# A softmax over rows of 512: ten transfers in place of sixteen, and a new order on VectorE

## The chip, the cores and the metric

The kernel runs on one core of one Trainium2 chip. The core has five engines that run side by side: TensorE (PE, not used here), VectorE (DVE), ScalarE (ACT), GpSimd (POOL) and SyncE (SP), which here only issues transfers. Transfers between the large memory (HBM) and the on-chip buffer (SBUF, 128 partitions) are carried out by 16 DMA engines, each of which works through the packets of eight partitions in the order in which SP issued the transfers.

The metric is the device time of one execution in microseconds. Each kernel is timed several times; the median counts.

## The reference

```python
def setup_inputs():
    batch, seq, dim = 16, 1024, 512
    return {"x": np.random.randn(batch, seq, dim).astype(np.float32)}

def reference(x):
    x_max = np.max(x, axis=-1, keepdims=True)
    exp_x = np.exp(x - x_max)
    return (exp_x / np.sum(exp_x, axis=-1, keepdims=True)).astype(np.float32)
```

There are 16,384 rows of 512 floats (2 KB each). Every row is read once and written once: 33.55 MB in, 33.55 MB out.

## The kernel before, in words

The rows are cut into 8 chunks. In a chunk every partition holds 16 rows that follow each other in HBM, 32 KB in one run, so a chunk is 128 x 16 rows, 4.19 MB. The buffer `held` has six places for chunks; chunks 6 and 7 take the places of chunks 0 and 1 once these are stored. A chunk is worked in two groups of 8 rows per partition, so there are 16 groups, and every instruction of VectorE and GpSimd handles one group.

A group goes through four steps:

- maximum (`rowmax`, line 133, VectorE): the negated maximum of each of the 8 rows. The first group of a chunk waits for the chunk's load.
- exponential (line 165, ScalarE): eight instructions, one for each row of the group; each subtracts the maximum, takes the exponential in place and sums it. After the eighth the semaphore `expd` goes up by one.
- reciprocal of the sums (line 142, VectorE), which waits for `expd`.
- multiply in place (line 144): on GpSimd for groups 0 to 11, on VectorE for the groups in `ON_VECTOR`, 12 to 15. It waits for the reciprocal. A chunk's store waits until both of its groups are multiplied.

No scheduler decides the order; it is written out for each engine. SP issues, in this order, the loads of chunks 0 to 5 (line 112, the first ahead of the program's opening barrier), stores 0 to 2, loads 6 and 7 (line 124, each after the store of the chunk whose place it takes), stores 3 to 7 (line 127). SP stands still at each wait, and whatever is behind in its list stands too. VectorE runs the maximum of group g, then the reciprocal of group g-1 and, where it is VectorE's, the multiply of g-1. ScalarE and GpSimd take groups in order. The two loops of ScalarE (`exps`) are there because the place in `held` starts again after 12 groups.

`take` (line 94) is a wait for a semaphore that also takes the count down, so the profile names line 94 wherever an engine waits.

Of the kernel before, what the change touches and what calls it, by code (L numbers as in the profile page):

```python
# [1 line left out]

# [4 lines left out]

F32 = mybir.dt.float32
EXP = mybir.ActivationFunctionType.Exp
AX = mybir.AxisListType.X  # L10

CHUNK = 16
CHUNKS = 8
PLACES = 6
GROUP = 8
PER = CHUNK // GROUP
GROUPS = CHUNKS * PER
RING = PLACES * PER  # L20


ORDER = [("L", k) for k in range(PLACES)] + [
    ("S", 0),
    ("S", 1),
    ("S", 2),
    ("L", 6),
    ("L", 7),
    ("S", 3),
    ("S", 4),  # L30
    ("S", 5),
    ("S", 6),
    ("S", 7),
]


ON_VECTOR = (12, 13, 14, 15)


AT_HEAD = {mybir.EngineType.SP: 1}  # L40

def loads_at_the_head(nc):

    main, body = nc.main_func.blocks[0], nc.main_func.blocks[1]
    for engine, count in AT_HEAD.items():
        loads = [
            i
            for i in body.instructions  # L50
            if i.engine == engine and type(i).__name__ == "InstDMACopy"
        ][:count]
        barrier = next(
            n
            for n, i in enumerate(main.instructions)
            if i.engine == engine and type(i).__name__ == "InstDrain"
        )
        for load in loads:
            body.instructions.remove(load)
        main.instructions[barrier:barrier] = loads  # L60


@with_exitstack
def kernel(
    ctx: ExitStack,
    tc: tile.TileContext,
    x: bass.AP,
    out: bass.AP,
):
    nc = tc.nc  # L70
    nc.at_finalize(loads_at_the_head)
    P = nc.NUM_PARTITIONS

    x_rows = x.flatten_outer_dims().rearrange("(c p r) d -> c p r d", p=P, r=CHUNK)
    out_rows = out.flatten_outer_dims().rearrange("(c p r) d -> c p r d", p=P, r=CHUNK)
    n, _, _, d = x_rows.shape
    assert n == CHUNKS

    held = nc.alloc_sbuf_tensor("held", [P, PLACES * CHUNK, d], F32).ap()
    shift = nc.alloc_sbuf_tensor("shift", [P, GROUPS * GROUP], F32).ap()  # L80
    sums = nc.alloc_sbuf_tensor("sums", [P, GROUPS * GROUP], F32).ap()
    recip = nc.alloc_sbuf_tensor("recip", [P, GROUPS * GROUP], F32).ap()

    loaded = [nc.alloc_semaphore(f"loaded{k}") for k in range(CHUNKS)]
    stored = [nc.alloc_semaphore(f"stored{k}") for k in range(CHUNKS)]
    maxed = nc.alloc_semaphore("maxed")
    expd = nc.alloc_semaphore("expd")
    to_pool = nc.alloc_semaphore("to_pool")
    to_vector = nc.alloc_semaphore("to_vector")
    scaled = [nc.alloc_semaphore(f"scaled{k}") for k in range(CHUNKS)]  # L90

    def take(engine, semaphore, n):

        engine.wait_ge(semaphore, n).then_inc(semaphore, -n)  # L94

    def place(k):
        at = (k % PLACES) * CHUNK
        return held[:, at : at + CHUNK, :]

    def rows(g):  # L100
        at = (g % RING) * GROUP
        return held[:, at : at + GROUP, :]

    def stats(t, g):
        return t[:, g * GROUP : (g + 1) * GROUP]

    with tc.manual_schedule():  # L110
        for _, k in ORDER[:PLACES]:
            first = nc.sync.dma_start(out=place(k), in_=x_rows[k])
            first.then_inc(loaded[k], 16)
            tc.no_tile_sem_insts.add(first.ins.name)
    tc.close()
    tc.compile()  # L116

    reused = set()
    for what, k in ORDER[PLACES:]:
        if what == "L":  # L120
            if k >= PLACES:
                take(nc.sync, stored[k - PLACES], 16)
                reused.add(k - PLACES)
            nc.sync.dma_start(out=place(k), in_=x_rows[k]).then_inc(loaded[k], 16)
        else:
            take(nc.sync, scaled[k], PER)
            nc.sync.dma_start(out=out_rows[k], in_=place(k)).then_inc(stored[k], 16)


    def rowmax(g):  # L130
        if g % PER == 0:
            take(nc.vector, loaded[g // PER], 16)
        nc.vector.reduce_max(  # L133
            out=stats(shift, g), in_=rows(g), axis=AX, negate=True
        ).then_inc(maxed, 1)

    def scale(g):
        engine, ready = (
            (nc.vector, to_vector) if g in ON_VECTOR else (nc.gpsimd, to_pool)
        )  # L140
        take(nc.vector, expd, 1)
        nc.vector.reciprocal(out=stats(recip, g), in_=stats(sums, g)).then_inc(ready, 1)  # L142
        take(engine, ready, 1)
        engine.tensor_mul(  # L144
            out=rows(g),
            in0=rows(g),
            in1=stats(recip, g).unsqueeze(2).to_broadcast([P, GROUP, d]),
        ).then_inc(scaled[g // PER], 1)

    for g in range(GROUPS):  # L150
        rowmax(g)
        if g:
            scale(g - 1)
    scale(GROUPS - 1)


    nc.scalar.preload_act_table(EXP)  # L157

    def exps(first, turns):
        with nc.scalar.Fori(0, turns) as i:  # L160
            take(nc.scalar, maxed, 1)
            for r in range(GROUP):
                row = held[:, bass.ds(i * GROUP + r, 1), :]
                at = bass.ds(i * GROUP + (first * GROUP + r), 1)
                act = nc.scalar.activation(  # L165
                    out=row,
                    in_=row,
                    func=EXP,
                    bias=shift[:, at],
                    scale=1.0,  # L170
                    accum_out=sums[:, at],
                )
            act.then_inc(expd, 1)

    exps(0, RING)
    exps(RING, GROUPS - RING)


    for k in range(CHUNKS):
        if k not in reused:  # L180
            take(nc.sync, stored[k], 16)


# [1 line left out]
_INS = ['x']  # L185
_OUTS = [((16, 1024, 512), 'float32')]


# [23 lines left out]
```

## Time and profile before

| | us |
|---|---|
| median of three runs | 160.24 (160.07 to 160.30) |
| the profiled execution's own time | 160.32 |
| its span, first to last instruction | 159.0 |
| VectorE busy | 90.6 |
| ScalarE busy | 92.0 |
| GpSimd busy | 84.0 |
| 16 maxima on VectorE, mean of one | 4.398 |
| 12 multiplies on GpSimd, mean of one | 7.018 |
| 4 multiplies on VectorE, mean of one | 4.576 |
| 128 exponentials, each with the read of its sum behind it, mean of one | 0.706 and 0.186 |

The span is what the trace of one execution covers; the device time holds a little more than the span. In the trace's rows, "busy" is the time in which an engine ran instructions; a transfer's "us to landing" goes from its issue on SP to the last of its semaphore updates, and so holds the time that it stood behind other transfers. The DMA share of a stretch is the packets' time over 16 engines' time; a packet's time and bytes are counted where it starts and ends, so in stretches of one microsecond both figures jump about, and a long stretch is steadier. "x" gives the number of instructions.

### The profile page before, as it was taken

Reading aid. Unit: us, or ns where it says so; the run is one execution under the profiler, and the core shown is the slowest. Engines: PE = TensorE matmul, PEld = TensorE weight load, DVE = VectorE, ACT = ScalarE, POOL = GpSimd, SP = SyncE. Lnnn points to the kernel's source line nnn. Section 1 sums busy time; section 2 is a strip of 40 time slices with the busy share of each in tenths; the row PEclk is TensorE's granted clock in tenths of the full one; section 3 lists DMA queues with packets and bytes.
Section 4 is the critical chain, followed back from the end, with each engine's and each line's share of the span. In section 5 each row is a group of like instructions: output and inputs, shape, how many; then the busy total and the mean of one; then the engine's idle time right before and its main releaser. Section 6 shows DMA issues by size and latency. Waiting matters only on the chain. (4 is left out here: it accounts for less than half of the span.)

```text
span 159.0 us, 740 instructions
## 1 busy us (share of the span) xinstructions
DVE 90.6 (57%) x36; ACT 92.0 (58%) x257; POOL 84.0 (53%) x16
## 2 busy tenths in 40 slices
DVE  0008959777977977887700000695999998740000
ACT  0300699999999999999993000059934929200000
POOL 0000009999999999999999999259200000000000
DMA  7999999999999999999999999999999999999995
GB/s 264 470 445 404 404 478 437 396 470 445 404 404 470 445 396 396 396 412 470 437 396 445 470 404 404 478 437 398 437 437 437 412 462 414 437 437 429 429 429 256
DMA packets 2306, 67.13 MB, mean 422 GB/s; under 512 B 256, under 2 KB 256, under 8 KB 256
## 3 DMA queue, kind: packets, MB, share of 16 engines
q1 hardware_dynamic: 2304, 67.11, 98.8%
q14 instruction: 2, 0.02, 0.0%
HBM read 33.55 MB, written 33.55 MB: 422 GB/s over the span
## 5 line engine op out<-in xcount | busy, mean ns | idle before, releaser
L165 ACT ACTIVATE held<-held,shift x128 | 90.3, 706 | 40.0 <-ACTq L94 40.0
L144 POOL TENSOR_TENSOR held<-held,recip 128x4096 f32<-128x4096 f32 x12 | 83.8, 7018 | 28.1 <-POOLq L94 28.1
L133 DVE TENSOR_REDUCE shift<-held 128x8 f32<-128x4096 f32 x16 | 70.3, 4398 | 33.3 <-DVEq L94 33.3
L165 ACT ACTIVATION_READ_ACCUMULATOR held<-held,shift x128 | 23.8, 186 | 0.0
L144 DVE TENSOR_TENSOR held<-held,recip 128x4096 f32<-128x4096 f32 x4 | 18.3, 4576 | 0.6
L142 DVE RECIPROCAL recip<-sums 128x8 f32<-128x8 f32 x16 | 3.2, 201 | 16.4 <-DVEq L94 16.4
L157 ACT ACT_TABLE_LOAD x1 | 1.3, 1283 | 4.0 <-PEq L116 4.0
L196 POOL MEMSET const-float32-0.0<- 128x1 f32 x1 | 0.1, 99 | 0.2 <-issue 0.2
L196 POOL MEMSET const-uint8-127<- 128x1 uint8 x1 | 0.1, 103 | 0.0
L196 POOL MEMSET const-bfloat16-1.0<- 128x1 bf16 x1 | 0.1, 102 | 0.0
L196 POOL MEMSET const-float32-1.0<- 128x1 f32 x1 | 0.1, 99 | 0.0
## 6 DMA issues: line engine op xcount, KB each, us to landing
held<-in_x_dram SPq DMA_DIRECT2D x8, 4096.0 KB, 29.9
out_dram<-held SPq DMA_DIRECT2D x8, 4096.0 KB, 28.3
```

What stands on the lines that cost most here:

```text
L133: nc.vector.reduce_max(out=stats(shift, g), in_=rows(g), axis=AX, negate=True).then_inc(maxed, 1)
L142: nc.vector.reciprocal(out=stats(recip, g), in_=stats(sums, g)).then_inc(ready, 1)
L144: engine.tensor_mul(out=rows(g), in0=rows(g), in1=stats(recip, g).unsqueeze(2).to_broadcast([P, GROUP, d]),).then_inc(scaled[g // PER], 1)
L157: nc.scalar.preload_act_table(EXP)
L165: act = nc.scalar.activation(out=row, in_=row, func=EXP, bias=shift[:, at], scale=1.0, accum_out=sums[:, at],)
L196: nc = _bacc.Bacc("TRN2", target_bir_lowering=False, num_devices=1)
```

## The change

Groups stay as they are, 8 rows per partition. The chunks go. In their place there are four blocks of four groups for the loads (`BLOCKS`: 32 rows per partition, 64 KB in one run, 8.39 MB) and six ranges of groups for the stores (`STORES`): groups 0 to 3 and 8 to 11 as 32 rows per partition, groups 4 and 5, 6 and 7, 12 and 13, 14 and 15 as 16 rows per partition each. Which rows a partition holds changes with it: a block gives each partition 32 consecutive rows, so the parts of neighbouring partitions lie 64 KB apart in HBM instead of 32, and a store of 16 rows writes half of such a part.

SP's list becomes: loads of groups 0-3, 4-7, 8-11; store 0-3; store 4-5; load 12-15 (after store 0-3 has landed, whose places it takes); store 6-7; store 8-11; store 12-13; store 14-15. In the changed file the loads are at line 109, the stores at line 131, the maximum at 140, the reciprocal at 146, the multiply at 148 and the exponential at 172.

VectorE's order is a written list: M is a maximum, P a reciprocal whose multiply GpSimd does, V a reciprocal and multiply on VectorE. Three maxima stand ahead of the first reciprocal; group 2 is now multiplied on VectorE, between the maximum of group 4 and the reciprocal of group 3; group 12, before on VectorE, goes to GpSimd. In number both engines keep theirs: 12 multiplies on GpSimd, 4 on VectorE. ScalarE's order is the same.

```diff
--- before.py
+++ after.py
@@ -11,30 +11,29 @@
 
 
 
-CHUNK = 16
-CHUNKS = 8
-PLACES = 6
 GROUP = 8
-PER = CHUNK // GROUP
-GROUPS = CHUNKS * PER
-RING = PLACES * PER
-
-
-ORDER = [("L", k) for k in range(PLACES)] + [
-    ("S", 0),
-    ("S", 1),
-    ("S", 2),
-    ("L", 6),
-    ("L", 7),
-    ("S", 3),
-    ("S", 4),
-    ("S", 5),
-    ("S", 6),
-    ("S", 7),
+GROUPS = 16
+RING = 12
+
+
+
+BLOCKS = [(0, 4), (4, 8), (8, 12), (12, 16)]
+STORES = [(0, 4), (4, 6), (6, 8), (8, 12), (12, 14), (14, 16)]
+AHEAD = BLOCKS[:3]
+ORDER = [
+    ("S", (0, 4)),
+    ("S", (4, 6)),
+    ("L", (12, 16)),
+    ("S", (6, 8)),
+    ("S", (8, 12)),
+    ("S", (12, 14)),
+    ("S", (14, 16)),
 ]
 
 
-ON_VECTOR = (12, 13, 14, 15)
+
+VECTOR = "M0 M1 M2 P0 M3 P1 M4 V2 P3 M5 P4 M6 P5 M7 P6 M8 P7 M9 P8 M10 P9 M11 P10 P11"
+VECTOR += " M12 M13 P12 M14 M15 V13 V14 V15"
 
 
 AT_HEAD = {mybir.EngineType.SP: 1}
@@ -71,87 +70,95 @@
     nc.at_finalize(loads_at_the_head)
     P = nc.NUM_PARTITIONS
 
-    x_rows = x.flatten_outer_dims().rearrange("(c p r) d -> c p r d", p=P, r=CHUNK)
-    out_rows = out.flatten_outer_dims().rearrange("(c p r) d -> c p r d", p=P, r=CHUNK)
-    n, _, _, d = x_rows.shape
-    assert n == CHUNKS
-
-    held = nc.alloc_sbuf_tensor("held", [P, PLACES * CHUNK, d], F32).ap()
+    d = x.shape[-1]
+    x_rows, out_rows = x.flatten_outer_dims(), out.flatten_outer_dims()
+    assert x_rows.shape[0] == GROUPS * GROUP * P
+
+    def in_dram(rows, a, b):
+
+        first, last = next(k for k in BLOCKS if k[0] <= a and b <= k[1])
+        block = rows[first * GROUP * P : last * GROUP * P]
+        block = block.rearrange("(p r) d -> p r d", p=P)
+        return block[:, (a - first) * GROUP : (b - first) * GROUP, :]
+
+    held = nc.alloc_sbuf_tensor("held", [P, RING * GROUP, d], F32).ap()
     shift = nc.alloc_sbuf_tensor("shift", [P, GROUPS * GROUP], F32).ap()
     sums = nc.alloc_sbuf_tensor("sums", [P, GROUPS * GROUP], F32).ap()
     recip = nc.alloc_sbuf_tensor("recip", [P, GROUPS * GROUP], F32).ap()
 
-    loaded = [nc.alloc_semaphore(f"loaded{k}") for k in range(CHUNKS)]
-    stored = [nc.alloc_semaphore(f"stored{k}") for k in range(CHUNKS)]
+    loaded = {k: nc.alloc_semaphore(f"loaded{k[0]}") for k in BLOCKS}
+    scaled = {k: nc.alloc_semaphore(f"scaled{k[0]}") for k in STORES}
+    stored = {k: nc.alloc_semaphore(f"stored{k[0]}") for k in STORES}
     maxed = nc.alloc_semaphore("maxed")
     expd = nc.alloc_semaphore("expd")
     to_pool = nc.alloc_semaphore("to_pool")
     to_vector = nc.alloc_semaphore("to_vector")
-    scaled = [nc.alloc_semaphore(f"scaled{k}") for k in range(CHUNKS)]
 
     def take(engine, semaphore, n):
 
         engine.wait_ge(semaphore, n).then_inc(semaphore, -n)
 
-    def place(k):
-        at = (k % PLACES) * CHUNK
-        return held[:, at : at + CHUNK, :]
-
-    def rows(g):
-        at = (g % RING) * GROUP
-        return held[:, at : at + GROUP, :]
+    def rows(a, b):
+        assert a // RING == (b - 1) // RING
+        return held[:, a % RING * GROUP : ((b - 1) % RING + 1) * GROUP, :]
 
     def stats(t, g):
         return t[:, g * GROUP : (g + 1) * GROUP]
 
+    def load(k):
+        copy = nc.sync.dma_start(out=rows(*k), in_=in_dram(x_rows, *k))
+        copy.then_inc(loaded[k], 16)
+        return copy
+
 
 
 
     with tc.manual_schedule():
-        for _, k in ORDER[:PLACES]:
-            first = nc.sync.dma_start(out=place(k), in_=x_rows[k])
-            first.then_inc(loaded[k], 16)
-            tc.no_tile_sem_insts.add(first.ins.name)
+        for k in AHEAD:
+            tc.no_tile_sem_insts.add(load(k).ins.name)
     tc.close()
     tc.compile()
 
     reused = set()
-    for what, k in ORDER[PLACES:]:
+    for what, k in ORDER:
         if what == "L":
-            if k >= PLACES:
-                take(nc.sync, stored[k - PLACES], 16)
-                reused.add(k - PLACES)
-            nc.sync.dma_start(out=place(k), in_=x_rows[k]).then_inc(loaded[k], 16)
+            free = (k[0] - RING, k[1] - RING)
+            take(nc.sync, stored[free], 16)
+            reused.add(free)
+            load(k)
         else:
-            take(nc.sync, scaled[k], PER)
-            nc.sync.dma_start(out=out_rows[k], in_=place(k)).then_inc(stored[k], 16)
+            take(nc.sync, scaled[k], k[1] - k[0])
+            nc.sync.dma_start(out=in_dram(out_rows, *k), in_=rows(*k)).then_inc(
+                stored[k], 16
+            )
 
 
     def rowmax(g):
-        if g % PER == 0:
-            take(nc.vector, loaded[g // PER], 16)
+        for k in BLOCKS:
+            if k[0] == g:
+                take(nc.vector, loaded[k], 16)
         nc.vector.reduce_max(
-            out=stats(shift, g), in_=rows(g), axis=AX, negate=True
+            out=stats(shift, g), in_=rows(g, g + 1), axis=AX, negate=True
         ).then_inc(maxed, 1)
 
-    def scale(g):
-        engine, ready = (
-            (nc.vector, to_vector) if g in ON_VECTOR else (nc.gpsimd, to_pool)
-        )
+    def scale(g, engine, ready):
         take(nc.vector, expd, 1)
         nc.vector.reciprocal(out=stats(recip, g), in_=stats(sums, g)).then_inc(ready, 1)
         take(engine, ready, 1)
         engine.tensor_mul(
-            out=rows(g),
-            in0=rows(g),
+            out=rows(g, g + 1),
+            in0=rows(g, g + 1),
             in1=stats(recip, g).unsqueeze(2).to_broadcast([P, GROUP, d]),
-        ).then_inc(scaled[g // PER], 1)
-
-    for g in range(GROUPS):
-        rowmax(g)
-        if g:
-            scale(g - 1)
-    scale(GROUPS - 1)
+        ).then_inc(next(scaled[k] for k in STORES if k[0] <= g < k[1]), 1)
+
+    for step in VECTOR.split():
+        what, g = step[0], int(step[1:])
+        if what == "M":
+            rowmax(g)
+        elif what == "V":
+            scale(g, nc.vector, to_vector)
+        else:
+            scale(g, nc.gpsimd, to_pool)
 
 
     nc.scalar.preload_act_table(EXP)
@@ -176,7 +183,7 @@
     exps(RING, GROUPS - RING)
 
 
-    for k in range(CHUNKS):
+    for k in STORES:
         if k not in reused:
             take(nc.sync, stored[k], 16)
 
```

## The prediction

> **What bounds the kernel now.** I read the page first: shares of busy time, the DMA rows of the slices, the DMA queue and the chain that ended last.
>
> ```profile
> DVE 90.6 (57%) x36; ACT 92.0 (58%) x257; POOL 84.0 (53%) x16
> ...
> DMA packets 2306, 67.13 MB, mean 422 GB/s; under 512 B 256, under 2 KB 256, under 8 KB 256
> ...
> q1 hardware_dynamic: 2304, 67.11, 98.8%
> ...
> DVE held L144 3%
> ```
>
> No engine is busy for 60% of the span; the one queue that carries all 67.11 MB is at 98.8%. The chain holds only 3% of the span because it does not go through transfers: the last multiply ends near 141 us, and behind it the last store waits its turn. So I asked for the transfers by line (issue to landing), and for rates in stretches, with a closer look where the page's GB/s row dips.
>
> ```profile
> DMA to landing us min/median/max: 12.3/35.2/58.7
> ...
> 57.00:58.00 1.00, 1.00 (x2) 1.00 (x3) 1.00 (x1) 1.00 1.18 492
> 58.00:59.00 1.00, 1.00 (x1) 1.00 (x5) 1.00 (x2) 1.00 1.46 393
> 59.00:60.00 1.00, 1.00 (x1) 1.00 (x3) 1.00 (x1) 1.00 0.60 164
> 60.00:61.00 1.00, 1.00 (x1) 1.00 (x5) 1.00 (x1) 1.00 0.92 393
> 61.00:62.00 1.00, 0.52 (x1) 1.00 (x4) 1.00 (x1) 1.00 0.76 328
> 62.00:72.00 10.00, 8.24 (x4) 10.00 (x29) 10.00 (x2) 1.00 1.02 439
> 139.00:149.00 10.00, 1.93 (x1) 0.00 (x0) 0.00 (x0) 1.00 1.00 433
> ```
>
> The first line is the six early loads: the first is in at 12.3 us, the sixth, issued at 2.8, at 61.5. The undisturbed rate is the last row, 433 GB/s: with 2048 packets of 32 KB on 16 DMA engines that is 32,768 x 16 / 433 = 1.21 us a packet, 9.68 us a 4.19 MB transfer (eight packets on each engine). Sixteen such transfers are 154.9 us; the other 4.1 of the 159.0 are 2.3 of start, 0.5 from the last byte to its semaphore, and about 1.3 of disturbance, the largest the pause at 59, when the last load turns into the first store. The packet records behind these rows show it: the last load packets end 0.6 to 1.0 us late, for the whole queue about 0.75 us. The turn at 109 us costs 0.3 on the slowest engine, the turn from stores to loads at 90 nothing.
>
> The third reading is the order of VectorE and GpSimd, which decides when stores can start.
>
> ```profile
> 12.48 8.74 DVE L133 TENSOR_REDUCE shift<-held 128x8 f32<-128x4096 f32 x2 [12.48 <-DVEq L94]
> 23.10 0.20 DVE L142 RECIPROCAL recip<-sums 128x8 f32<-128x8 f32 x1 [1.88 <-DVEq L94]
> 23.56 76.77 POOL L144 TENSOR_TENSOR held<-held,recip 128x4096 f32<-128x4096 f32 x11 [23.12 <-POOLq L94]
> 37.65 28.23 SPq L127 DMA_DIRECT2D out_dram<-held  x3
> 105.31 7.02 POOL L144 TENSOR_TENSOR held<-held,recip 128x4096 f32<-128x4096 f32 x1 [4.99 <-POOLq L94]
> 111.58 5.03 DVE L144 TENSOR_TENSOR held<-held,recip 128x4096 f32<-128x4096 f32 x1
> 121.19 4.42 DVE L144 TENSOR_TENSOR held<-held,recip 128x4096 f32<-128x4096 f32 x1
> ```
>
> A maximum takes 4.4 us, a group of exponentials 5.64 (the spacing of the reciprocals), a multiply 6.98 on GpSimd and 4.42 on VectorE. The one at 111.58 took 5.03: GpSimd was inside its own until 112.33, and VectorE ended 4.28 after that, as if it had stood still for the overlap. Today the first store is issued at 37.65, 23 us before the queue can take it.
>
> **The change part by part.** *Bytes*: the same, so 154.9 us stay. *Fewer, larger pieces*: a partition's part of a 32-row transfer is 64 KB in one run. If that is one packet, as 32 KB is now, each engine handles 80 packets in place of 128 (loads 64 to 32, the two large stores 32 to 16, the others 32 as before). The price of a packet boundary is bounded by the trace's two sizes: 8 KB instruction packets took 309 ns, 32 KB ones 1213; on that line 8 ns are fixed, and since packets start 3 to 4 ns before their predecessors end, 5 remain. So 48 x 5 = 0.24 us less; below, 0 if 64 KB is cut in two again; above, 48 x 8 = 0.38. I take 5. Half of it lies before the first store, where it buys nothing if the queue then waits, so 0.12 counts. *Six fewer issues* (0.34 us each on SP): SP waits 150 us of the span, nothing; the cover is the filled queue. *Semaphores and fewer waits of VectorE*: loaded four times in place of eight, nothing on the path.
>
> Here I weigh a page's rule. In the rows, transfers follow each other with no gap, so a transfer has no price of its own while another is queued. The Trainium skill's page "DMA: Bandwidth & Descriptors", section "Anatomy of one DMA", fits a fixed 2.0 us per DMA beside its bytes; six fewer would be 12 us less by that fit, some 147 us. The trace disagrees for queued transfers, since sixteen times 2.0 us do not fit into the 4.1 us above.
>
> *First data later.* The first block is twice as large and lands at 22.0 (12.3 + 9.7); the whole chain moves by 9.7 us. *The first store*, (0,4), needs four groups. Step by step: M0 22.2 to 26.5; exponentials from 26.9 in steps of 5.64; P0's reciprocal at 32.8, GpSimd on P0 33.3 to 40.2 and P1 to 47.2; M4 waits for the second block (41.4), 41.6 to 46.0; V2's reciprocal 46.1, its multiply ready at 46.4 but held by P1 to 47.2, ending 47.2 + 4.28 = 51.5; only then P3's reciprocal, behind it on VectorE; GpSimd on P3 51.9 to 58.9; the store is issued at 59.0 (0.1 behind, as 37.65 is behind 37.52). The loads run out at 59.6 to 60.3, engine by engine, if the pause goes, and at 60.5 to 61.1 if it stays. How long a store takes from issue to flowing data on an idle queue no row shows. The nearest is the first load: its first packets start 1.0 to 1.9 us after issue, and data flow as if from 1.6 (first engine) to 2.3 (last). By it the slowest engine starts the store at 61.3, against 61.15 now: +0.13. The other end is a store that arrives just in time after loads with no pause: 60.3, -0.85. The load row contains the wait for HBM data, which a store reading the on-chip buffer should not have in full, so I take the middle, -0.36. Whether the pause belongs to the turn itself (reading ahead for a queued store while loads still land) is an assumption.
>
> *The other stores have cover.* P5 ends near 72.8, wanted 80.5. (0,4) lands near 80.7, so the last load is issued about 9 us before its turn at 90. P7 86.8, wanted 109.7. P11 114.7, wanted 119.4. The last block lands at 110.2: M12 to 114.8, exponentials 115.1 to 137.7, P12 121.3 to 128.4, V13 130.0 to 134.4, V14 to 139.4, V15 139.9 to 144.3; wanted 138.7 and 148.4. The thinnest cover here is 4 us (of which starting from idle would need up to 2.3); it hides GpSimd's eleven multiplies in a row and VectorE's last three.
>
> *Sum*: 158.99 - 0.12 - 0.36 = 158.5 us of span. The profiled execution took 160.32, 1.33 more than its span, and lies 0.08 above the median of 160.24; so 158.5 + 1.25 = 159.8 us.
>
> **The rivals.** *The pause is the loads' own* and stays: the loads then end at 61.0, the store is ready by 60.6 to 61.3, nothing is won there but the 0.12: 160.1. For it: it strikes all engines within a microsecond, before any store is written. Against: the turn at 109 has a small one too, and no other place has.
>
> *The first store is late* (the other sign). Place: P3 behind V2 behind P1, then the start from idle. From an issue later than about 59.3 with the load's 2.3 us of start, every microsecond of delay is one of time, since nothing else is queued at 61. A delay of 0.9 more (as much again as V2 stands held) gives 160.24 + 0.13 - 0.12 + 0.9 = 161.2. For it: the margin is negative or a few tenths. Against: each duration in the chain is steady (eleven multiplies in 76.77 us).
>
> *64 KB steps between partitions move slower.* Now the parts of neighbouring partitions lie 32 KB apart in HBM, afterwards 64. From 2.43 us a packet of 64 KB on (2 x 1.21 and 0.2% more) the gain is gone; 1% on all of it is 1.5 us, 161.5. No row here has another spacing; that loads and stores both keep 1.21 us speaks for a limit elsewhere. The Trainium skill's page "DMA: Bandwidth & Descriptors", section "Latency and other measured facts", tells of rates falling at large power-of-two row pitches, but from 2 MiB on, and lists 512 KiB as 207 GB/s against 214 for a padded pitch; no run here shows it, and it puts 64 KB on the safe side.
>
> *Both gains in full*: no pause, a store that starts at once, 0.24 to 0.38: 159.0 to 159.2. *A transfer has a price even when queued*: the nearest row is the 0.3 us turn; six of them, 1.8 less, 158.4.
>
> **How the numbers follow.** A comparison of this kernel can tell about 0.2%, 0.32 us, from no change. The forecast has 0.45, its own range 159.3 to 160.3 (transition from -0.85 to +0.13): 0.30 of that below 159.92, 0.15 within. The pause that stays: 0.17, within. Late first store: 0.18, slower. Slower pieces: 0.10, slower. Both gains in full 0.07 and a price per transfer 0.03, faster. Faster 0.40, same 0.32, slower 0.28. The range, 159.2 to 161.2, leaves out the faster two in part and the tails of the slower two.
>
> **What would show it.** 1280 data packets (and 160 of semaphores) in place of 2048, the large ones taking 2.42 us; first maximum near 22.2, V2 ending near 51.5, GpSimd's third multiply 51.9 to 58.9, the first store issued at 59.0; rates without the dip to 164 at 59, or with a short gap at 60 to 61; all other stores issued ahead of their turn. Wrong would make it: the first store issued after 59.5; a large packet over 2.43 us; a second gap before 120 or 139.

## The result: 1.8% slower

The changed kernel took 163.07 us at the median of four runs (162.91 to 163.28) against 160.18 of the kernel before on the same chip: a ratio of 1.0176, 95% interval 1.0161 to 1.0191. The profiled execution took 163.15 with a span of 161.8. The forecast was 159.8, its range 159.2 to 161.2.

The page of the changed kernel, in parts that were shown of the kernel before (busy time, the packets, the DMA queue):

```profile
DVE 92.7 (57%) x36; ACT 91.9 (57%) x257; POOL 84.0 (52%) x16
...
DMA packets 1442, 67.13 MB, mean 415 GB/s; under 512 B 160, under 2 KB 160, under 8 KB 160
...
q1 hardware_dynamic: 1440, 67.11, 97.4%
```

The same bytes in 1280 data packets, as forecast, but the queue's share fell from 98.8% to 97.4%, and the mean rate from 422 to 415 GB/s. The rates in stretches of one microsecond (columns: stretch, its length, busy time of DVE, ACT and POOL with their instructions, PE clock, DMA share, GB/s) show where the queue stood empty:

```profile
59.00:60.00 1.00, 1.00 (x1) 1.00 (x4) 1.00 (x1) 1.00 0.01 0
60.00:61.00 1.00, 1.00 (x1) 1.00 (x5) 1.00 (x1) 1.00 0.00 0
61.00:62.00 1.00, 1.00 (x1) 1.00 (x3) 1.00 (x2) 1.00 0.00 0
62.00:63.00 1.00, 0.69 (x1) 1.00 (x5) 1.00 (x1) 1.00 2.46 1049
```

The order of VectorE, GpSimd and SP shows why, in the lines that answer to those of before:

```profile
22.19 13.07 DVE L140 TENSOR_REDUCE shift<-held 128x8 f32<-128x4096 f32 x3 [22.19 <-DVEq L99]
35.18 0.19 DVE L146 RECIPROCAL recip<-sums 128x8 f32<-128x8 f32 x1
46.19 7.71 DVE L148 TENSOR_TENSOR held<-held,recip 128x4096 f32<-128x4096 f32 x1
35.62 13.99 POOL L148 TENSOR_TENSOR held<-held,recip 128x4096 f32<-128x4096 f32 x2 [35.19 <-POOLq L99]
54.19 62.81 POOL L148 TENSOR_TENSOR held<-held,recip 128x4096 f32<-128x4096 f32 x9 [4.57 <-POOLq L99]
61.30 14.29 SPq L131 DMA_DIRECT2D out_dram<-held  x2
```

The first reciprocal comes at 35.18, behind three maxima that run without a break, though its sums were ready near 32.8. GpSimd's first two multiplies end at 49.61; VectorE's multiply of group 2, at hand since 46.19, ends 4.29 after that; the fourth group is done at 61.2, and the first store is issued at 61.30. The loads had run out at 59.7 to 60.4.

A second loss is further on, at the turns: a turn is the place in the queue where loads end and stores begin, or the other way round. The transfers' rate in three long stretches of the changed kernel:

```profile
62.20:88.00 25.80, 19.43 (x11) 25.80 (x74) 25.80 (x4) 1.00 1.00 429
88.00:113.00 25.00, 3.98 (x3) 10.22 (x30) 25.00 (x5) 1.00 0.99 398
113.00:158.00 45.00, 31.17 (x11) 22.69 (x64) 11.01 (x2) 1.00 1.00 431
```

In the middle stretch, which holds the turn from stores to loads (near 91) and back (near 111), the rate is 7% lower. By the packet records the last packets ahead of the turns (and the first behind the earlier one) take 0.94 and 0.87 us longer than their kind, taken as a mean over the engines; in the kernel before these two turns cost nothing and 0.08.

The balance, as means over the 16 engines: the loads end 1.03 earlier (59.85 in place of 60.88: no pause at 59, fewer packets); the queue is empty for 2.35 in place of nothing; from the first store to the end it takes 98.73 in place of 97.01, 1.72 more. Together +3.04; the slowest engine, which sets the end, loses 2.86 of that.

### The profile page after: what moved, and what is told of

It is laid out like the page before. It is cut to its first block, busy times and chain, and to the rows that moved or that the text cites. A ratio compares the mean times of both kernels' runs of the same rounds, so it can differ in the third digit from the quotient of the medians.

```text
span 161.8 us, 726 instructions
## 1 busy us (share of the span) xinstructions
DVE 92.7 (57%) x36; ACT 91.9 (57%) x257; POOL 84.0 (52%) x16
## 3 DMA queue, kind: packets, MB, share of 16 engines
q1 hardware_dynamic: 1440, 67.11, 97.4%
## 5 line engine op out<-in xcount | busy, mean ns | idle before, releaser
L148 DVE TENSOR_TENSOR held<-held,recip 128x4096 f32<-128x4096 f32 x4 | 21.0, 5246 | 0.6
```

The lines of the kernel that those rows point to most:

```text
L148: engine.tensor_mul(out=rows(g, g + 1), in0=rows(g, g + 1), in1=stats(recip, g).unsqueeze(2).to_broadcast([P, GROUP, d]),).then_inc(next(s ...
```

## The experiments

**Undo one detail of VectorE's list**

```diff
-VECTOR = "M0 M1 M2 P0 M3 P1 M4 V2 P3 M5 P4 M6 P5 M7 P6 M8 P7 M9 P8 M10 P9 M11 P10 P11"
+VECTOR = "M0 M1 P0 M2 P1 M3 M4 V2 P3 M5 P4 M6 P5 M7 P6 M8 P7 M9 P8 M10 P9 M11 P10 P11"
```

> The changed kernel with VectorE's list begun as M0 M1 P0 M2 P1 M3 M4 V2 (before: M0 M1 M2 P0 M3 P1 M4 V2): the third maximum no longer stands ahead of the first reciprocal. Theory (the first store is late because of the third maximum, and every microsecond of it is one of time): first reciprocal at 32.8 instead of 35.2, multiply of group 2 ending at 52.1 instead of 53.9, first store issued at 59.7 instead of 61.3, its first packets 0.85 behind at 60.5, the end 1.6 earlier: 161.4 to 161.6. Rival (the delay of the first store is made up or replaced later, at the two turns near 90 and 110): 162.3 or more.

Measured: 161.31 us, 1.0074 (1.0060 to 1.0088) of the kernel before. SP and VectorE in this version:

```profile
32.56 0.20 DVE L146 RECIPROCAL recip<-sums 128x8 f32<-128x8 f32 x1 [1.88 <-DVEq L99]
47.28 4.42 DVE L148 TENSOR_TENSOR held<-held,recip 128x4096 f32<-128x4096 f32 x1
59.11 14.29 SPq L131 DMA_DIRECT2D out_dram<-held  x2
```

The third maximum was worth 2.2 us of the first store's issue and 1.76 of the time. The store came 0.6 us earlier than I expected, the time lies 0.1 under the range, and the rival's 162.3 did not come. It is also, by accident, the kernel that the prediction described: its first store is issued at 59.1 where the prediction had 59.0. Loads and store now meet with a mean gap of 0.19 us. Still it is 1.1 us above the kernel before, and by the packet records the two later turns cost 0.94 and 0.98 again. The stretch that holds the second of them (its rate is rough, since 64 KB packets are counted where they start and end):

```profile
105.00:112.00 7.00, 0.38 (x1) 0.00 (x0) 7.00 (x2) 1.00 0.84 304
```

So the empty stretch is not the whole loss.

**The first store in two**

```diff
-STORES = [(0, 4), (4, 6), (6, 8), (8, 12), (12, 14), (14, 16)]
+STORES = [(0, 2), (2, 4), (4, 6), (6, 8), (8, 12), (12, 14), (14, 16)]
...
-    ("S", (0, 4)),
+    ("S", (0, 2)),
+    ("S", (2, 4)),
```

The last load waits for both stores.

> The changed kernel with its first store cut in two (groups 0-1 and 2-3, 16 rows each), VectorE's list as in the changed kernel. The store of groups 0-1 is issued near 49.8, so it is queued when the loads run out near 60. Theory (the empty queue between 60 and 62 costs about 2.0 us, and the pause of the kernel before at 59 belongs to a queued store): no gap, a pause of about 0.75 in its place, 161.7 to 162.0. Rival A (the pause belonged to something else): no gap and no pause, 160.9 to 161.2. Rival B (the gap is not what costs): 162.8 or more.

Measured: 160.37 us, 1.0014 (1.0005 to 1.0023). None of the three had it. The first store is issued at 49.6; there is no gap, and there is a pause at 60, 1.29 us as a mean over the engines. What nobody had expected: the later turns cost nothing and 0.08, though everything behind the first two stores stands as in the changed kernel. The same three stretches:

```profile
62.20:88.00 25.80, 19.43 (x11) 25.80 (x73) 25.80 (x4) 1.00 1.02 442
88.00:113.00 25.00, 6.26 (x4) 10.06 (x30) 25.00 (x5) 1.00 0.98 423
113.00:158.00 45.00, 28.73 (x11) 22.68 (x64) 10.88 (x2) 1.00 1.00 431
```

423 GB/s in the middle in place of 398: 25 us at 398 carry what 23.5 carry at 423. So whether the later turns cost hangs on what happened at 60.

**The transfers alone, sixteen and ten.** In the kernel before and in the changed one all computation is cut out, and a store waits for a load (shown for the kernel before):

```diff
-            take(nc.sync, scaled[k], PER)
+            take(nc.sync, loaded[k], 16)
...
-    for g in range(GROUPS):
-        rowmax(g)
...
-    exps(RING, GROUPS - RING)
```

> The transfers of the kernel before alone, sixteen of 16 rows, in its order on SP; all computation is left out, so the output is the input, and a store waits only for its load. The queue is never empty. Theory A (the turns between loads and stores cost time by the transfers alone): the first turn near 59 shows again 0.7 us, that near 109 0.3, that near 90 nothing; 160.1 to 160.3. Theory B (they cost time because engines use the buffer beside them): no turn costs anything, 159.0 to 159.3.

> The transfers of the changed kernel alone, ten, in its order on SP; all computation is left out, so the output is the input, and a store waits only for the load of its block (the two second stores of a block for nothing). The queue is never empty. Theory A (a turn with a 64 KB piece on one side costs about 0.9 by the transfers alone): the turns near 90 and 110 show it again, and the first one too since its store is queued; 161.0 to 161.9, longer than the sixteen transfers alone by about 1 or more. Theory B (the cost of the turns comes from the engines' work beside): 158.8 to 159.0, 0.24 us shorter than the sixteen transfers alone.

Measured: sixteen transfers 159.71 us, 0.9968 (0.9957 to 0.9980) of the kernel before; ten transfers 160.17 us, 0.9999 (0.9985 to 1.0014). Neither theory had it right. With a filled queue the first turn pauses with no engine at work (0.77 us with sixteen, 1.11 with ten; theory B falls), the turns near 90 and 110 are free (at most 0.07; theory A falls, 64 KB pieces or not). And ten transfers are not shorter than sixteen by the 0.24 us of their fewer packets but longer by 0.5. The 0.24 is there, a 64 KB packet takes 2.418 in place of twice 1.213, but the larger pause (0.34 more) eats it. That accounts for 0.1 of the 0.5; in the two profiles the slowest engine, which sets the end, ends 0.27 later with ten. The rest is open.

**The transfers alone, with the queue empty once.** The theory that was left: it is the empty queue at the first turn that makes later turns cost. In both, the first store waits for the last early load too (shown for the sixteen, against the version above):

```diff
+            if k == 0:
+                nc.sync.wait_ge(loaded[5], 16)
             take(nc.sync, loaded[k], 16)
```

> The sixteen transfers alone, as in the run with all computation left out (the output is the input), but the first store also waits for the sixth load: the queue runs empty at 60 once, for some 2 us. Theory (an engine's reading runs ahead of its writing once the first turn with a filled queue has been paid for; an empty queue takes that lead away, and then each later turn between loads and stores costs about 0.9): first store from 62.4 on, no pause at 59, about 0.9 lost near 91 and again near 111; 162.4 to 162.9. Rival (the later turns cost because a 64 KB piece stands at them, the gap has nothing to do with it): no loss near 91 and 111, 160.9 to 161.3.

> The ten transfers alone (the output is the input), but the first store also waits for the third load: the queue runs empty at 60, first store from 61.7 on. Theory (an empty queue makes the later turns cost): no pause at 60, about 0.9 lost near 90 and 110 each, as in the changed kernel; 161.8 to 162.4. Rival (the loss near 90 and 110 in the changed kernel came from the engines' work): no loss there, 160.2 to 160.6.

Measured: 162.66 us with sixteen transfers, 1.0150 (1.0128 to 1.0171), and 162.56 with ten, 1.0144 (1.0120 to 1.0169). The turns cost 0.80 and 1.04 with sixteen, 0.88 and 1.03 with ten, and there is no pause at 59. The theory's numbers were met (the ten a little above the range), both rivals fall. Five stretches of the sixteen transfers with the empty queue (here POOL is the only engine that shows):

```profile
62.50:89.00 26.50, 0.00 (x0) 1.00 1.02 435
89.00:94.00 5.00, 0.00 (x0) 1.00 0.89 315
94.00:108.00 14.00, 0.00 (x0) 1.00 1.04 449
108.00:114.00 6.00, 0.00 (x0) 1.00 0.98 350
114.00:158.00 44.00, 0.00 (x0) 1.00 0.99 429
```

And without it, the sixteen transfers with a filled queue: the pause stands at 59, the turns at 90 and 110 don't show.

```profile
57.00:62.00 5.00, 0.00 (x0) 1.00 1.03 380
62.00:88.00 26.00, 0.00 (x0) 1.00 1.00 431
88.00:93.00 5.00, 0.00 (x0) 1.00 0.97 419
93.00:108.00 15.00, 0.00 (x0) 1.00 1.02 441
108.00:113.00 5.00, 0.00 (x0) 1.00 1.01 433
```

**More turns, with a filled queue and after an empty one.** Load 7 goes behind store 3, which makes five turns in place of three; the second version has the wait for the sixth load as well.

```diff
     ("L", 6),
+    ("S", 3),
     ("L", 7),
-    ("S", 3),
     ("S", 4),
```

> The sixteen transfers alone (the output is the input), queue always filled, with load 7 moved behind store 3: five turns between loads and stores instead of three. Theory (with a filled queue only the first turn is paid): 0.7 near 60, no more than 0.1 at each of the four others; 159.6 to 159.9, as the sixteen transfers in their old order. Rival (every turn from loads to stores costs 0.3 to 0.7): 160.2 or more.

> The sixteen transfers alone (the output is the input) in the order with five turns, and the first store waits for the sixth load as well, so that the queue is empty once near 61. Theory A (what the empty queue took away is built up again once and then lasts): the turns near 91 and 101 cost 0.8 to 1.0 each, those near 111 and 121 nothing; 162.6 to 163.0. Theory B (after an empty queue every turn is paid): all four cost about 0.9; 164.2 to 164.8.

Measured: filled, 160.01 us (0.9997, 0.9975 to 1.0019); only the first turn shows in the packet records (0.80 us), the other four do not. The time lies 0.1 above the range given (one of the ten executions took 161.65, the others at most 160.07); the span of the profiled execution, 158.6, is that of the three turns. After an empty queue, 162.80 us (1.0164, 1.0148 to 1.0179): the turns near 91 and 101 cost 0.89 and 0.81, those near 111 and 121 nothing, which is theory A. Stretches of the second version; the fourth and fifth turn lie in the last two:

```profile
88.00:98.00 10.00, 0.00 (x0) 1.00 0.97 380
98.00:108.00 10.00, 0.00 (x0) 1.00 1.02 406
108.00:118.00 10.00, 0.00 (x0) 1.00 0.98 423
118.00:155.00 37.00, 0.00 (x0) 1.00 1.01 438
```

So the rule that these runs show: the first turn from loads to stores on a filled queue costs 0.7 to 1.3 us once, and the turns behind it are free. If the queue runs empty there, that turn has no pause, but the next two are paid with 0.8 to 1.0 each. With the gap of 0.19 us in the first experiment this held as well.

There is a rival that none of the expectations had. After an empty queue the 16 engines start the first store almost together, within 0.14 to 0.27 us, and with a filled one within 0.53 to 0.76; the later turns could cost because the engines then turn in step. Against it: in the first experiment the engines stood 0.71 apart ahead of the turn near 106, as far as with a filled queue, and that turn cost 0.98 all the same. No run changes this spread alone.

**Why is the pause at 60 larger with the changed kernel's transfers?** First try: the third load, the one ahead of the turn, in two halves of 16 rows, in the version with the first store in two.

```diff
-AHEAD = BLOCKS[:3]
+LOADS = [(0, 4), (4, 8), (8, 10), (10, 12), (12, 16)]
+AHEAD = LOADS[:4]
```

> The version with the first store in two, and the third load in two halves of 16 rows as well (the rows' places in HBM and the buffer stay). The last packets before the turn at 60 are now 32 KB. Theory (the pause at 60 grows with the piece that stands last before the turn: 0.7 for 32 KB, 1.1 to 1.3 for 64 KB): pause back to 0.75, 159.8 to 160.0. Rival (it does not depend on the last piece): 160.3 to 160.5, as with the first store in two alone.

Measured: 160.51 us, 1.0013 (1.0001 to 1.0026), pause 1.18 us, and all pieces at that turn were of 32 KB. The rival holds: the length of the last pieces isn't it. Second try: the sixteen transfers alone, with the rows laid out as in the changed kernel.

```diff
-    x_rows = x.flatten_outer_dims().rearrange("(c p r) d -> c p r d", p=P, r=CHUNK)
+    x_rows = x.flatten_outer_dims().rearrange("(c p h r) d -> c h p r d", p=P, h=2, r=CHUNK)
...
-            first = nc.sync.dma_start(out=place(k), in_=x_rows[k])
+            first = nc.sync.dma_start(out=place(k), in_=x_rows[k // 2, k % 2])
```

The later loads and the stores are changed in the same way.

> The sixteen transfers of 16 rows alone (the output is the input), in their old order with a filled queue, but the rows laid out as in the changed kernel: the parts of neighbouring partitions lie 64 KB apart in HBM. Theory (the larger pause at 60 with the changed kernel's layout, 1.1 to 1.3 in place of 0.7, comes from the spacing): 1.1 to 1.3 at 60; 160.1 to 160.4. Rival (it comes from the length of the pieces): 0.7, 159.6 to 159.8.

Measured: 160.06 us, 0.9989 (0.9979 to 0.9998), and a pause of 1.06 us. Both lie a little under the theory's ranges, the time 0.3 above the rival's, though its interval just touches that of the sixteen transfers in their own layout. The stretch of the pause in this run carries 321 GB/s where the sixteen transfers in their own layout (shown above) carry 380:

```profile
57.00:62.00 5.00, 0.00 (x0) 1.00 0.96 321
```

Over all profiles with a filled queue at 60 the two layouts stand apart: 0.70 to 0.83 us in the four with a spacing of 32 KB (0.83 in the kernel before, 0.70 with VectorE's list alone, below), 1.06 to 1.29 in the four with 64 KB. So the layout with 64 KB between neighbouring partitions makes the pause larger, by 0.3 us in the one pair that differs in nothing else, each with one profile; why, no run shows. The time alone would not tell it: with five turns the sixteen transfers in their own layout took 160.01. Away from the turns the spacing costs nothing: 64 KB packets take 2.418 us throughout.

**The two parts of the change, each alone.** VectorE's list on the kernel before, and the ten transfers with VectorE's old order:

```diff
-ON_VECTOR = (12, 13, 14, 15)
+VECTOR = "M0 M1 M2 P0 M3 P1 M4 V2 P3 M5 P4 M6 P5 M7 P6 M8 P7 M9 P8 M10 P9 M11 P10 P11"
+VECTOR += " M12 M13 P12 M14 M15 V13 V14 V15"
...
-    for g in range(GROUPS):
-        rowmax(g)
-        if g:
-            scale(g - 1)
-    scale(GROUPS - 1)
+    for step in VECTOR.split():
+        what, g = step[0], int(step[1:])
...
```

```diff
-VECTOR = "M0 M1 M2 P0 M3 P1 M4 V2 P3 M5 P4 M6 P5 M7 P6 M8 P7 M9 P8 M10 P9 M11 P10 P11"
-VECTOR += " M12 M13 P12 M14 M15 V13 V14 V15"
+VECTOR = "M0 M1 P0 M2 P1 M3 P2 M4 P3 M5 P4 M6 P5 M7 P6 M8 P7 M9 P8 M10 P9 M11 P10 M12 P11 M13 V12 M14 V13 M15 V14 V15"
```

> One part of the change alone: the kernel before with VectorE's written list (M0 M1 M2 P0 M3 P1 M4 V2 and so on, group 2 on VectorE and group 12 on GpSimd), the sixteen transfers as they were. Theory (the list harms only where the first store needs four groups): the first store is issued near 41 instead of 37.7, the second near 53, both long before the loads run out at 60, so the time of the kernel before, 160.1 to 160.4. Rival (the list itself costs, by the held multiply of 7.7 us or at the end): 161 or more.

> The other part alone: the changed kernel's ten transfers with VectorE's order of the kernel before (group 2 on GpSimd, 12 on VectorE). Theory (the first store of four groups is late under either order): four multiplies in a row on GpSimd, 33.3 to 61.2, first store issued at 61.3 as in the changed kernel, empty queue from 60 to 62, about 0.9 lost at each of the turns near 91 and 111; 162.8 to 163.3. Rival (the new list is to blame): 161.5 or less.

Measured: the list alone 160.30 us, 1.0008 (0.9999 to 1.0017), no difference that can be told; its multiply of group 2 is held for even longer (8.67 us), and the first store, at 41.2, still has 19 us in hand. The transfers alone 167.50 us, 1.0459 (1.0445 to 1.0474). The first half of what I expected came: first store at 61.1, an empty queue (2.2 us as a mean over the engines), 0.88 and 0.99 lost at the later turns. A second hole I had not seen:

```profile
113.10 4.42 DVE L139 TENSOR_REDUCE shift<-held 128x8 f32<-128x4096 f32 x1 [23.90 <-DVEq L98]
117.44 0.19 DVE L145 RECIPROCAL recip<-sums 128x8 f32<-128x8 f32 x1
117.81 7.02 POOL L147 TENSOR_TENSOR held<-held,recip 128x4096 f32<-128x4096 f32 x1 [8.02 <-POOLq L98]
```

In the old order the reciprocal of group 11 stands behind the maximum of group 12, which waits for the last load (in at 113). Now that groups 8 to 11 leave in one store, that store waits with it, is issued at 124.9, and the queue is empty again, 3.8 us as a mean. The new list (P10 P11 ahead of M12) is what keeps the changed kernel from this. So the transfers are to blame and the list is not: it mends more than it harms, except for the third maximum.

No version here beats the kernel before. Its own sixteen transfers with no computation take 159.71, 0.3% less, so beside these transfers the engines' work costs hardly anything.

## Why the prediction was wrong

- *What bounds the kernel* held: the queue is the limit, and the time is 154.9 us of bytes and what is lost around them.
- *Fewer, larger pieces* held in the packets (1280; 2.418 us, the price of a boundary 5 to 8 ns as read off two sizes).
- *The first store* is the step that failed first, in "exponentials from 26.9 in steps of 5.64; P0's reciprocal at 32.8". VectorE's list has M2 ahead of P0; M2 runs from 30.9 to 35.2, so the reciprocal cannot come at 32.8. The maximum that I counted for three groups of exponentials I did not count for the engine that had to run it. Everything behind moved by 2.3 us: V2 ended at 53.9 (51.5 forecast), the store was issued at 61.3 (59.0). The order could be read from the list in the diff. All the other durations of that chain held, the held multiply too (49.61 + 4.29). There the Trainium skill's page "SBUF — State Buffer", section "Who interferes with whom", says that a VectorE instruction with two inputs in the buffer contends with a GpSimd instruction that reads it, through ports that they share under an exclusive lock; the trace agrees, 7.71 us in place of 4.42.
- *From issue to flowing data on an idle queue* was mis-sized the other way: 1.6 to 2.3 us by the nearest row, a first load. Measured from idle: the first packets 0.85 us after the issue began (61.30 to 62.15; the issuing instruction itself takes 0.35 of that) and only 0.03 to 0.05 longer than others. The Trainium skill's page "DMA: Bandwidth & Descriptors", section "Latency and other measured facts", gives about 0.6 us to the first byte; nearer than my row, and the measurement stands. The two errors partly cancelled: 2.3 late and 1 early.
- *The pause at 59* "belongs to the turn itself" was an assumption, and it held: without a queued store the loads ended on time in every run, and with one every run had the pause.
- *The other stores have cover* held for their issues: all came ahead of their turns. But the sum took it that a turn with cover costs what it had cost before, nothing near 90 and 0.3 near 109. That is the second step that failed: the change at these turns was put at nothing, from a kernel whose queue is always filled. In the first experiment, which has the issue time that I had worked out, the queue is empty for a mean of 0.19 us, and the kernel is still at 161.3, outside the forecast's own range: some 0.9 at each later turn. For the changed kernel that is 1.7 of the loss. In the terms of the sum, as means over the engines: the first store's data start 1.32 us later than in the kernel before, where the sum had 0.48 earlier, and all behind takes 1.72 longer, where the sum had nothing.
- Of the rivals, *the first store is late* is the one that came, with its place right (P3 behind V2 behind P1) and its price too low: 0.9 us where the empty queue was 2.35, and the later turns were not in it. The rival of the 64 KB spacing was wrong in its rule (no packet was slower) but has a grain of truth: a larger pause at the first turn, by 0.3 us. *A transfer has a price even when queued* had no sign in any run. The 2.0 us that the prediction quotes from the Trainium skill's page "DMA: Bandwidth & Descriptors" stand there in the section "Anatomy of one DMA — SWDGE (gpsimd) path", which is on transfers issued by GpSimd; here SyncE issues them.

## What to carry to other kernels

When a queue of transfers is the limit, a joined store waits for the work of all its parts: count on each engine, instruction by instruction in its written order, when it can be issued, and compare that with the time at which the queue runs out. "Just in time" is too late: a queue that runs empty for even 0.2 us was paid for again at two later turns, so the next transfer has to be queued well before the last one ends. Issued at 59.1 it was too late, at 49.6 early enough, with loads that ran out near 60; no run lies between. Fewer, larger transfers gained only the boundaries between packets, some 0.24 us here, and the layout that came with them cost 0.3 at the first turn.

## What was not expected of the hardware

- With a filled queue the first turn from loads to stores pauses all DMA engines (0.70 to 0.83 us for 32 KB spacing, 1.06 to 1.29 for 64 KB), with or without work on the engines, and later turns in both directions are free (five turns: 0.80 us in all). After an empty queue the next two turns cost 0.8 to 1.0 each and those behind them nothing. It looks as if reading got ahead of writing once and kept that lead until the queue ran dry; that picture foretold the runs with an empty queue to within 0.2 us, but no run shows the lead itself, and what it is stays open.
- A store issued on an idle queue moves its first packet 0.85 us later, at full rate at once (2.45 us for the first packet of 64 KB, 2.42 for the others).
